# Average pooling over 8192 rows: larger loads, grouped stores and a last group cut into pieces

## The chip, the cores and the metric

The kernel runs on one core of a Trainium2 chip. The metric is the device time of one execution in microseconds (us), as a median of several runs. All results use runs in the fast state alone; the granted clock was 1.0 in every profile. The profile's span is about 2 us shorter than the device time; times inside a profile count from the start of its span. DVE is the vector engine, ACT the scalar engine, Pool is GpSimd, and SP is the engine that issues the loads.

## The reference

Each row of 4096 floats is averaged in 256 windows of 16:

```python
# x: (32, 256, 4096) float32, output_size = 256
for i in range(output_size):
    start = int(i * length / output_size)
    end = int((i + 1) * length / output_size)
    result[:, :, i] = np.mean(x[:, :, start:end], axis=-1)
```

There are 32 x 256 = 8192 rows. 134.2 MB are read and 8.4 MB written, and every element takes part in one addition.

## The kernel before

One tile is 128 rows, one row per partition. A tile is loaded (2 MB, 16 KB per partition), reduced on DVE, scaled on ACT and stored (128 KB, 1 KB per partition). There are 64 tiles and four buffers of each kind. SP issues the loads and ACT the stores.

```python
    xin = ctx.enter_context(tc.tile_pool(name="xin", bufs=4))
    res = ctx.enter_context(tc.tile_pool(name="res", bufs=4))

    for i in range(n_tiles):            # 64
        # ... r0, r1 = i * 128, (i + 1) * 128; nr = 128; K = 16; O = 256 ...
        xt = xin.tile([P, O, K], mybir.dt.float32)
        nc.sync.dma_start(out=xt[:nr], in_=x_flat[r0:r1].rearrange("p (o k) -> p o k", k=K))

        rt = res.tile([P, O], mybir.dt.float32)
        nc.vector.tensor_reduce(out=rt[:nr], in_=xt[:nr],
                                axis=mybir.AxisListType.X, op=mybir.AluOpType.add)
        ot = res.tile([P, O], mybir.dt.float32)
        nc.scalar.mul(out=ot[:nr], in_=rt[:nr], mul=inv_k)

        nc.scalar.dma_start(out=out_flat[r0:r1], in_=ot[:nr])
```

## Time and profile before

| what | value |
|---|---|
| device time, median | 345.52 us (345.41 to 345.62) |
| span of the profile | 343.8 us |
| DVE busy | 82% |
| steady traffic | 428 GB/s, DMA engines fully busy |
| from the last load's landing to the end of the span | 7.5 us |

The page of the kernel before, cut: busy time by engine, DMA share and rate in 40 slices, DMA queues, the chain that ended last, the costliest group and the DMA issues.

```profile
DVE 282.9 (82%) x64; ACT 27.9 (8%) x65; POOL 0.2 (0%) x4
...
DMA  8999999999999999999999999999999999999991
...
DMA packets 18437, 142.65 MB, mean 415 GB/s; under 512 B 2049, under 2 KB 10241, under 8 KB 10241
...
q1 hardware_dynamic: 9216, 134.22, 91.4%
q10 hardware_dynamic: 9216, 8.39, 7.0%
...
DMA xt<-in_x_dram 77%; DVE rt L48 21%; SPq L45 0%; ACT ot L55 0%; DVEq L48 0%
...
L48 DVE TENSOR_REDUCE rt<-xt 128x256 f32<-128x4096 f32 x64 | 282.9, 4420 | 58.0 <-DMA xt<-in_x_dram 58.0
...
xt<-in_x_dram SPq DMA_DIRECT2D x64, 2048.0 KB, 16.3
out_dram<-ot ACTq DMA_DIRECT2D x64, 128.0 KB, 10.2
```

The DMA row has a 9 in every slice but the first and the last: the DMA engines never rest. DVE is 82% busy, and the end of its group line says that it waited 58.0 us for loads. So DMA bounds the body. The two queues, q1 for loads and q10 for stores, take 91.4% and 7.0% of the engines' time, together nearly all of it. A load takes 16.3 us from issue to landing, although one lands every 5.2 us: about three are always queued.

Windows of the kernel before (stretch in us, its length, busy time of DVE, ACT and Pool, clock, DMA share, GB/s):

```profile
80.00:120.00 40.00, 33.71 (x9) 3.33 (x8) 0.00 (x0) 1.00 1.01 428
120.00:160.00 40.00, 33.69 (x9) 3.33 (x8) 0.00 (x0) 1.00 1.01 428
```

The end of the chain of waits of the kernel before (start in us, length in us, what):

```profile
320.05 16.29 DMA xt<-in_x_dram
...
336.43 4.43 DVE rt L48
340.86 0.02 issue
340.88 0.42 ACT ot L55
```

The last load lands at 336.34. Then one reduce, one scaling and one store follow in series. In the trace's records of single packets the last read packet ends at 336.00.

### The profile page before, as it was taken

How to read it: one execution, taken by the hardware profiler on the slowest of the kernel's cores; microseconds unless marked ns; L12 is line 12 of the kernel's file. 1: busy time of each engine (PE TensorE's matmuls, PEld its weight loads, DVE VectorE, ACT ScalarE, POOL GpSimd, SP SyncE). 2: the span in 40 equal slices, each digit the busy share in tenths (PEclk: the TensorE clock that was granted, in tenths of full speed). 3: DMA queues.
4: the chain of work that ended last, by engine and by line, in shares of the span. 5: the costliest groups of instructions: out<-in, count | busy, mean ns of one | idle time of the engine just before them, and what ended most of it. 6: DMA issues, size and time to landing. Idle time of an engine off the chain costs nothing.

```text
span 343.8 us, 484 instructions
## 1 busy us (share of the span) xinstructions
DVE 282.9 (82%) x64; ACT 27.9 (8%) x65; POOL 0.2 (0%) x4
## 2 busy tenths in 40 slices
DVE  0988988988888888889879889888888888898895
ACT  1000000000000000000000000000000000000000
POOL 0000000000000000000000000000000000000000
DMA  8999999999999999999999999999999999999991
GB/s 305 429 421 433 433 426 425 425 430 433 427 423 423 436 430 425 424 425 435 430 424 424 426 436 425 426 425 431 432 425 427 423 431 431 427 425 426 430 417 43
DMA packets 18437, 142.65 MB, mean 415 GB/s; under 512 B 2049, under 2 KB 10241, under 8 KB 10241
## 3 DMA queue, kind: packets, MB, share of 16 engines
q1 hardware_dynamic: 9216, 134.22, 91.4%
q10 hardware_dynamic: 9216, 8.39, 7.0%
q14 instruction: 5, 0.03, 0.0%
HBM read 134.22 MB, written 8.39 MB: 415 GB/s over the span
## 4 chain that ended last, share of the span: by engine, by line
DMA 77%; DVE 21%; issue 0%; SPq 0%; ACT 0%; DVEq 0%
DMA xt<-in_x_dram 77%; DVE rt L48 21%; SPq L45 0%; ACT ot L55 0%; DVEq L48 0%
## 5 line engine op out<-in xcount | busy, mean ns | idle before, releaser
L48 DVE TENSOR_REDUCE rt<-xt 128x256 f32<-128x4096 f32 x64 | 282.9, 4420 | 58.0 <-DMA xt<-in_x_dram 58.0
L55 ACT ACTIVATE ot<-rt 128x256 f32<-128x256 f32 x64 | 26.6, 416 | 312.7 <-DVE rt L48 312.7
L55 ACT ACT_TABLE_LOAD x1 | 1.3, 1283 | 0.7 <-PEq L74 0.7
L74 POOL MEMSET const-bfloat16-1.0<- 128x1 bf16 x1 | 0.1, 103 | 0.0
L74 POOL MEMSET const-uint8-127<- 128x1 uint8 x1 | 0.1, 102 | 0.0
L74 POOL MEMSET const-float32-0.0<- 128x1 f32 x1 | 0.1, 100 | 0.2 <-issue 0.2
L74 POOL MEMSET const-float32-1.0<- 128x1 f32 x1 | 0.1, 99 | 0.0
## 6 DMA issues: line engine op xcount, KB each, us to landing
xt<-in_x_dram SPq DMA_DIRECT2D x64, 2048.0 KB, 16.3
out_dram<-ot ACTq DMA_DIRECT2D x64, 128.0 KB, 10.2
```

The costliest lines, as they stand in the source:

```text
L48: nc.vector.tensor_reduce(out=rt[:nr], in_=xt[:nr], axis=mybir.AxisListType.X, op=mybir.AluOpType.add,)
L55: nc.scalar.mul(out=ot[:nr], in_=rt[:nr], mul=inv_k)
L74: nc = _bacc.Bacc("TRN2", target_bir_lowering=False, num_devices=1)
```

## The change

The intent is threefold. Eight neighbouring rows go to one partition, so that a load takes two rows per partition (32 KB, 4 MB in all). Eight rows of results are scaled by one instruction and stored by one transfer (8 KB per partition, 1 MB). The last group is cut so that little is left after the last load: 2 MB chunks, then nine pieces from 1 MB down to 128 KB, with stores in between.

```diff
+    R = 8
+    W = 2
+    S = R // W
+    x_g = x_flat.rearrange("(g p r) l -> g p (r l)", p=P, r=R)
+    o_g = out_flat.rearrange("(g p r) o -> g p (r o)", p=P, r=R)
     xin = ctx.enter_context(tc.tile_pool(name="xin", bufs=4))
-    res = ctx.enter_context(tc.tile_pool(name="res", bufs=4))
+    res = ctx.enter_context(tc.tile_pool(name="res", bufs=2))
 ...
+            # load_slot(s): W rows of every partition, one load, one reduce
+            xt = xin.tile([P, W * L], FP, name="xt")
+            nc.sync.dma_start(out=xt, in_=x_g[g, :, base:base + W * L])
+            nc.vector.tensor_reduce(out=rt[:, s * W * O:(s + 1) * W * O], ...)
 ...
+        def store(r0, r1):
+            nc.scalar.mul(out=ot[:, r0 * O:r1 * O], in_=rt[:, r0 * O:r1 * O], mul=inv_k)
+            nc.scalar.dma_start(out=o_g[g, :, r0 * O:r1 * O], in_=ot[:, r0 * O:r1 * O])
+
+        if not last:
+            for s in range(S):
+                load_slot(s)
+            store(0, R)
+        else:
+            for s in range(S - 2):
+                load_slot(s, tail_chunks=[L, L])
+            store(0, R - 4)
+            load_slot(S - 2, tail_chunks=[L, L])
+            store(R - 4, R - 2)
 ...
+            for ne in (L // 2, L // 4, L // 4):      # piece: load ne elements, reduce them
+                piece(e, e + ne); e += ne
+            store_cols(0, O)
+            for ne in (L // 4, L // 4):
+                piece(e, e + ne); e += ne
+            store_cols(O, O + O // 2)
+            for ne in (L // 4, L // 8, L // 16, L // 16):
+                piece(e, e + ne); e += ne
+            store_cols(O + O // 2, 2 * O)
```

(Cut and joined in places; the arithmetic is the same.)

More of the change, by code (lines that the diff above doesn't have):

```diff
@@ L19 @@
     P = nc.NUM_PARTITIONS
+    FP = mybir.dt.float32
     B, C, L = x.shape
@@ L31, with reduce_cols @@
     out_flat = out.flatten_outer_dims()
-    n_tiles = (rows + P - 1) // P
     inv_k = 1.0 / K
-    xin = ctx.enter_context(tc.tile_pool(name="xin", bufs=4))
-    res = ctx.enter_context(tc.tile_pool(name="res", bufs=4))
-    for i in range(n_tiles):
-        r0 = i * P
-        r1 = min(r0 + P, rows)
-        nr = r1 - r0
-        xt = xin.tile([P, O, K], mybir.dt.float32)
-        nc.sync.dma_start(out=xt[:nr], in_=x_flat[r0:r1].rearrange("p (o k) -> p o k", k=K))
-        rt = res.tile([P, O], mybir.dt.float32)
+    R = 8
+    W = 2
+    S = R // W
+    rows_per_group = P * R
+    n_groups = rows // rows_per_group
+    assert n_groups * rows_per_group == rows
+    x_g = x_flat.rearrange("(g p r) l -> g p (r l)", p=P, r=R)
+    o_g = out_flat.rearrange("(g p r) o -> g p (r o)", p=P, r=R)
+    xin = ctx.enter_context(tc.tile_pool(name="xin", bufs=4))
+    res = ctx.enter_context(tc.tile_pool(name="res", bufs=2))
+    def reduce_cols(xt, rt, r, cs, ce):
         nc.vector.tensor_reduce(
-            out=rt[:nr],
-            in_=xt[:nr],
+            out=rt[:, cs:ce],
+            in_=xt[:, cs * K:ce * K].rearrange("p (o k) -> p o k", k=K),
             axis=mybir.AxisListType.X,
@@ L53, with load_slot, piece, store_cols @@
         )
-        ot = res.tile([P, O], mybir.dt.float32)
-        nc.scalar.mul(out=ot[:nr], in_=rt[:nr], mul=inv_k)
-        nc.scalar.dma_start(out=out_flat[r0:r1], in_=ot[:nr])
+    for g in range(n_groups):
+        last = g == n_groups - 1
+        rt = res.tile([P, R * O], FP, name="rt", tag="rt")
+        ot = res.tile([P, R * O], FP, name="ot", tag="ot")
+        def load_slot(s, tail_chunks=None):
+            xt = xin.tile([P, W * L], FP, name="xt")
+            base = s * W * L
+            if tail_chunks is None:
+                nc.sync.dma_start(out=xt, in_=x_g[g, :, base:base + W * L])
+                nc.vector.tensor_reduce(
+                    out=rt[:, s * W * O:(s + 1) * W * O],
+                    in_=xt.rearrange("p (o k) -> p o k", k=K),
+                    axis=mybir.AxisListType.X,
+                    op=mybir.AluOpType.add,
+                )
+            else:
+                e0 = 0
+                for ne in tail_chunks:
+                    e1 = e0 + ne
+                    nc.sync.dma_start(
+                        out=xt[:, e0:e1], in_=x_g[g, :, base + e0:base + e1]
+                    )
+                    nc.vector.tensor_reduce(
+                        out=rt[:, s * W * O + e0 // K:s * W * O + e1 // K],
+                        in_=xt[:, e0:e1].rearrange("p (o k) -> p o k", k=K),
+                        axis=mybir.AxisListType.X,
+                        op=mybir.AluOpType.add,
+                    )
+                    e0 = e1
+                assert e0 == W * L
+        def store(r0, r1):
+            nc.scalar.mul(
+                out=ot[:, r0 * O:r1 * O], in_=rt[:, r0 * O:r1 * O], mul=inv_k
+            )
+            nc.scalar.dma_start(
+                out=o_g[g, :, r0 * O:r1 * O], in_=ot[:, r0 * O:r1 * O]
+            )
+        if not last:
+            for s in range(S):
+                load_slot(s)
+            store(0, R)
+        else:
+            for s in range(S - 2):
[3 more added lines that the diff above has]
+            store(R - 4, R - 2)
+            xt = xin.tile([P, W * L], FP, name="xt")
+            base = (S - 1) * W * L
+            rbase = (S - 1) * W * O
+            def piece(e0, e1):
+                nc.sync.dma_start(
+                    out=xt[:, e0:e1], in_=x_g[g, :, base + e0:base + e1]
+                )
+                nc.vector.tensor_reduce(
+                    out=rt[:, rbase + e0 // K:rbase + e1 // K],
+                    in_=xt[:, e0:e1].rearrange("p (o k) -> p o k", k=K),
+                    axis=mybir.AxisListType.X,
+                    op=mybir.AluOpType.add,
+                )
+            def store_cols(c0, c1):
+                nc.scalar.mul(
+                    out=ot[:, rbase + c0:rbase + c1],
+                    in_=rt[:, rbase + c0:rbase + c1],
+                    mul=inv_k,
+                )
+                nc.scalar.dma_start(
+                    out=o_g[g, :, (R - 2) * O + c0:(R - 2) * O + c1],
+                    in_=ot[:, rbase + c0:rbase + c1],
+                )
+            e = 0
+            for ne in (L // 2, L // 4, L // 4):
+                piece(e, e + ne)
+                e += ne
+            store_cols(0, O)
+            for ne in (L // 4, L // 4):
+                piece(e, e + ne)
+                e += ne
+            store_cols(O, O + O // 2)
+            for ne in (L // 4, L // 8, L // 16, L // 16):
+                piece(e, e + ne)
+                e += ne
+            assert e == W * L
+            store_cols(O + O // 2, 2 * O)
```

## The prediction

> **What bounds the kernel now.** DMA. The windows view gives a DMA share of 1.01 and about 428 GB/s (402.6 read, 25.1 written) in every steady stretch. DVE is busy 82% but waits on loads before every reduce (58.0 us, groups view). The chain of waits is 77% DMA; its 21% of DVE are reduces freeing buffers, harmless because 16.3 us of loads are always queued (issue to landing). Only the ends are serial: the last load lands at 336.34, then reduce 4.42, mul 0.42, store to the end at 343.85: 7.5 us of tail.
>
> **What changes.** The same 134.2 MB are read, 8.4 MB written and as many elements reduced.
>
> 1. Packets. The trace's packets are regular: 16 KB read 611 ns, 1 KB write 46 ns, 4 B semaphore 9 ns. The line through these has about 8 ns fixed per packet and a slope equal to 435 GB/s on 16 engines, the fabric ceiling in the Trainium skill, "DMA: Bandwidth & Descriptors", section Specifications. Before the first store, reads alone run at 431.2 GB/s; from that and the steady mix, writes are worth 380 GB/s. Stores of 8 KB per partition should go near 430: 2.6 us saved over 8.39 MB. If 32 KB rows go as one packet, the reads save up to 1.4 us more; if split at 16 KB, nothing. Estimate: 2.6 to 4 us off the DMA stream, all critical.
>
> 2. Tail. The last pieces are small (the last reduce is 128x256 elements), which looks like saving 4 us. I expect less, because DVE is nearly as slow as DMA: 4.45 us against 5.1 us per 2 MB. When the last 2 MB chunk before the pieces lands, DVE still owes it 4.45 us plus 8192 elements in nine reduces. With 1.04 ns an element (0.96 GHz, Trainium skill, "Trainium Kernel Development and Optimization", section NeuronCore Architecture; that leaves 0.15 of 4.42 us as fixed cost) these take about 10.3 us: 14.7 in all. DMA needs 9.7 us for the last 4 MB, 0.4 for the pieces' packets and some 1.6 for held-back stores: 11.8 us. So DVE ends about 3 us after the last load lands, not 0.5; before it was 4.5. The last mul and store are half as big: 0.1 us. Saving about 1.6 us.
>
> 3. No cost expected: the first reduce starts at about 13 us rather than 8.6, but DVE has slack (8.7 us per 10.3 us load), and four 4 MB buffers keep two loads queued. Fewer DMA issues and muls are off the path.
>
> Sum: 4.2 to 5.6 us off 345.5. Predicted 340.6 us (-1.4%), range 338.3 to 343.2. Faster by over 2% 0.13, within 2% 0.82, slower 0.05.
>
> **What would show it.** Step 1: steady windows at 430 to 433 GB/s; 8 KB write packets near 310 ns; about 7,900 packets, or 11,500 if split; last load landing at 332.5 to 334. Step 2: no DVE idle in the last 10 us, last reduce ending 2 to 4 us after the last landing; within 1 us, step 2 is wrong. Step 3: no DMA gap before the tail.
>
> **What would make it wrong.** Each partition's row in HBM now lies 128 KB from the next rather than 16 KB. The skill's DMA page (section Latency and other measured facts) shows large power-of-two pitches slowing DMA from 512 KiB up; no trace here shows one. If it bites at 128 KB, the kernel is slower. On the other side, bunched stores that make loads land later in the tail would let DVE catch up, saving 2 us more; and writes overlapping reads could lift the stream to 435 GB/s, just over the 2% line.

## The result

The changed kernel takes 340.66 us (340.47 to 340.80, 7 runs) against 345.52 us. The ratio is 0.9859, with a 95% interval of 0.9849 to 0.9869; that is clearly faster. Ratios in this document are the mean time of one kernel's fast runs over that of the other's fast runs of the same rounds, so they are not quite the ratio of the medians.

The page of the changed kernel, the lines that answer to those above:

```profile
DVE 278.5 (82%) x43; ACT 17.4 (5%) x13; POOL 0.2 (0%) x4
...
DMA  7999999999999999999999999999999999999994
...
DMA packets 7920, 142.61 MB, mean 421 GB/s; under 512 B 880, under 2 KB 1520, under 8 KB 2544
...
q1 hardware_dynamic: 6192, 134.22, 92.6%
q10 hardware_dynamic: 1728, 8.39, 6.0%
...
L67 DVE TENSOR_REDUCE rt<-xt 128x512 f32<-128x8192 f32 x28 | 243.2, 8686 | 55.4 <-DMA xt<-in_x_dram 55.4
...
xt<-in_x_dram SPq DMA_DIRECT2D x28, 4096.0 KB, 32.5
...
out_dram<-ot ACTq DMA_DIRECT2D x7, 1024.0 KB, 16.0
```

There are 7,920 packets in place of 18,437. The DMA engines are as full as before, DVE is as busy and waits as long. The body is bound by the same thing and moves its bytes a little faster. The same windows of the changed kernel:

```profile
80.00:120.00 40.00, 33.53 (x5) 1.91 (x1) 0.00 (x0) 1.00 1.00 433
120.00:160.00 40.00, 33.49 (x5) 1.91 (x1) 0.00 (x0) 1.00 1.00 433
```

The tail of the changed kernel, from its timeline (start, length, engine, line, operation, shapes, count, idle time before it):

```profile
321.94 4.42 DVE L80 TENSOR_REDUCE rt<-xt 128x256 f32<-128x4096 f32 x1 [0.68 <-DMA xt<-in_x_dram]
326.27 9.15 DVE L117 TENSOR_REDUCE rt<-xt 128x128 f32<-128x2048 f32 x9
...
335.46 0.31 ACT L125 ACTIVATE ot<-rt 128x128 f32<-128x128 f32 x1 [2.06 <-DVE rt L117]
335.80 0.34 ACTq L130 DMA_DIRECT2D out_dram<-ot  x1
```

Read the two DVE lines together. The reduce at 321.94 takes the last 2 MB chunk and waits 0.68 us for it. The nine reduces of the pieces follow with no idle time in brackets: their data was always there first. The last read packet ends at 333.32, the last reduce at 335.44, the span at 338.5. So the last 2.1 us of DVE work are a backlog, not a wait for the last piece. The trace's semaphore events say the same: the last piece was reported as landed at 333.76, and its reduce began at 335.02.

By the packet records, the last load came 2.7 us earlier (336.00 to 333.32) and the stretch behind it became 2.6 us shorter (7.8 to 5.2). The span fell by 5.3 us and the device time by 4.9; the gap between span and device time grew from 1.8 to 2.1 us. In the profiled runs below that gap is either 1.7 to 1.8 or 2.1 to 2.2 us (1.7 in `e8`, which has the same loads and stores), so it can't be put down to the change; nothing here explains it.

### The profile page after: what moved, and what is told of

Its sections match the earlier page's. It is cut to its first block, busy times and chain, and to the rows that moved or that the text cites. A ratio compares the mean times of both kernels' runs of the same rounds, so it can differ in the third digit from the quotient of the medians.

```text
span 338.5 us, 207 instructions
## 1 busy us (share of the span) xinstructions
DVE 278.5 (82%) x43; ACT 17.4 (5%) x13; POOL 0.2 (0%) x4
## 2 busy tenths in 40 slices
DMA packets 7920, 142.61 MB, mean 421 GB/s; under 512 B 880, under 2 KB 1520, under 8 KB 2544
## 4 chain that ended last, share of the span: by engine, by line
DMA 76%; DVE 22%; SPq 0%; DVEq 0%; issue 0%; ACT 0%
DMA xt<-in_x_dram 76%; DVE rt L67 18%; DVE rt L117 3%; DVE rt L80 1%; SPq L66 0%; DVEq L179 0%; SPq L77 0%; ACT ot L125 0%
## 5 line engine op out<-in xcount | busy, mean ns | idle before, releaser
L67 DVE TENSOR_REDUCE rt<-xt 128x512 f32<-128x8192 f32 x28 | 243.2, 8686 | 55.4 <-DMA xt<-in_x_dram 55.4
L90 ACT ACTIVATE ot<-rt 128x2048 f32<-128x2048 f32 (+2 forms) x9 | 15.1, 1673 | 310.0 <-DVE rt L67 285.2
L80 DVE TENSOR_REDUCE rt<-xt 128x256 f32<-128x4096 f32 x6 | 26.3, 4415 | 1.5 <-DMA xt<-in_x_dram 1.5
L117 DVE TENSOR_REDUCE rt<-xt 128x64 f32<-128x1024 f32 (+3 forms) x9 | 9.2, 1090 | 0.0
L125 ACT ACTIVATE ot<-rt 128x128 f32<-128x128 f32 (+1 forms) x3 | 1.0, 345 | 7.7 <-DVE rt L117 7.7
## 6 DMA issues: line engine op xcount, KB each, us to landing
xt<-in_x_dram SPq DMA_DIRECT2D x5, 512.0 KB, 15.8
```

Of the source, the lines that this page charges most:

```text
L67: nc.vector.tensor_reduce(out=rt[:, s * W * O:(s + 1) * W * O], in_=xt.rearrange("p (o k) -> p o k", k=K), axis=mybir.AxisListType.X, op=m ...
L80: nc.vector.tensor_reduce(out=rt[:, s * W * O + e0 // K:s * W * O + e1 // K], in_=xt[:, e0:e1].rearrange("p (o k) -> p o k", k=K), axis=my ...
L90: nc.scalar.mul(out=ot[:, r0 * O:r1 * O], in_=rt[:, r0 * O:r1 * O], mul=inv_k)
L117: nc.vector.tensor_reduce(out=rt[:, rbase + e0 // K:rbase + e1 // K], in_=xt[:, e0:e1].rearrange("p (o k) -> p o k", k=K), axis=mybir.Axis ...
L125: nc.scalar.mul(out=ot[:, rbase + c0:rbase + c1], in_=rt[:, rbase + c0:rbase + c1], mul=inv_k,)
```

## The experiments

Twelve kernels ran, all correct, each with the kernel before beside it (345.5 to 345.6 us in every round). Where packet times, landings or rates with two decimals are given, they come from the trace's records of single packets, with a packet's bytes spread evenly over its time. They are shown in tables, because the views give whole GB/s.

### Cutting only the tail of the kernel before

`e4` cuts the last tile of the kernel before into six pieces, `e5` the last two tiles into the same nine pieces that the change has. Nothing else is touched.

```diff
+        if i >= n_tiles - N_CUT:
+            for group in CUTS[i - (n_tiles - N_CUT)]:
+                # for each n of group: load n windows, reduce them; then scale and store the group
+    # e4: CUTS = [[[64, 64], [64, 32, 16, 16]]]
+    # e5: CUTS = [[[128, 64, 64]], [[64, 64], [64, 32, 16, 16]]]
```

> The kernel before with its last 2 MB tile alone cut into six loads, reduces and two stores; all else as before. Theory (DVE backlog): the tile ahead of it lands at 330.8 and its reduce ends at 335.65; then DVE works 4.75 us on the six pieces without a pause, last reduce at 340.4 against 340.86, half a store: about 345.0 us, DVE ending 4 us after the last load. Rival (only the last piece's reduce is serial): about 341.8 us.

> The kernel before with its last two tiles in the same nine pieces and three stores as the changed kernel's last slot. Theory (DVE backlog): the tile ahead has its reduce end at 330.4, the nine pieces take DVE 9.15 us as in the changed kernel, last reduce at 339.6, about 344.1 us. Rival (only the last piece's reduce is serial): about 341.8 us.

Measured: `e4` 344.90 us (ratio 0.9982, 0.9969 to 0.9994), `e5` 343.95 us (0.9952, 0.9940 to 0.9965). Both are as the backlog theory has it, and far from the 341.8 us of its rival. The timeline of `e4`:

```profile
331.20 4.42 DVE L71 TENSOR_REDUCE rt<-xt 128x256 f32<-128x4096 f32 x1 [0.79 <-DMA xt<-in_x_dram]
335.54 4.71 DVE L59 TENSOR_REDUCE rt<-xt 128x64 f32<-128x1024 f32 x6
```

DVE starts on the tile ahead at 331.20 and is not idle again until 340.25. The last read packet ended at 336.45, so 3.8 us of work were left at that moment, where the uncut kernel had 4.9 us until its reduce ended (336.00 to 340.86). DVE gains only some 0.8 us on DMA per 2 MB (the idle time of 0.79 in the first line), so cutting the last 2 MB cannot remove a backlog of one whole reduce. Cutting 4 MB removes more of it.

### Taking DVE work out of the tail

`e7` spreads the cuts over the whole last group. `e8` keeps the changed kernel and gives two pieces of 1024 elements to GpSimd, as four additions each.

```diff
 # e7: the last group
+            CUTS = [[[4096, 3584]], [[3072, 2560, 2048]], [[1024], [2048, 2048, 2048]],
+                    [[2048], [1536, 1536], [1024, 1024]], [[1024, 1024], [512, 256, 256]]]
 # e8: the second and the fourth piece
+                if pool:
+                    tree(e0, e1)      # four nc.gpsimd.tensor_tensor additions
+                    return
```

> The changed kernel with its whole last group in pieces that shrink slowly (4096 elements down to 256) and stores that follow. Theory (DVE backlog; smaller pieces leave less of it at each landing): last reduce ends about 1 us after the last landing rather than 2.1, about 339.7 us. Rival (the tail is bound by latency of landing and store, not by DVE): 340.7 us or slightly more for the extra packets.

> The changed kernel with two of the nine last pieces (1024 elements each) summed on GpSimd by four additions apiece, which takes 2.3 us of work from DVE and leaves loads and stores as they are. Theory (DVE backlog ends the kernel): the last reduce is then bound by the last landing, about 334.2 instead of 335.4, time about 339.4 us. Rival (landing and store latency): 340.7 us. If GpSimd takes longer than about 3 us for a piece, the middle store is late and the run says nothing of DVE.

Measured: `e7` 340.76 us (0.9859, 0.9846 to 0.9873), no gain. `e8` 340.00 us (0.9838, 0.9825 to 0.9852), about 0.65 us better than the changed kernel by the medians, half of what was expected; the two intervals overlap. By the spans of their profiles (338.3 and 338.5) it is only 0.2 us shorter; the rest lies in the unexplained gap between span and device time.

In `e7` the backlog did shrink, to 1.4 us behind the last read packet, but that packet came at 334.09 instead of 333.32. With 19 loads instead of 15 in the last group, the gain on DVE went back to DMA. Small pieces cost DMA time in the changed kernel too: from 327 to 330 us, where its pieces are 4 KB per partition, traffic runs at 409 GB/s.

The timeline of `e8`:

```profile
330.68 1.22 DVE L142 TENSOR_REDUCE rt<-xt 128x64 f32<-128x1024 f32 x1 [0.87 <-DMA xt<-in_x_dram]
...
332.34 2.46 DVE L142 TENSOR_REDUCE rt<-xt 128x64 f32<-128x1024 f32 x4 [0.44 <-DMA xt<-in_x_dram]
```

The brackets now have DMA in them: DVE waits for pieces, which it never did in the changed kernel. It ends at 334.80 instead of 335.44. So the backlog was what ended the changed kernel, and with it gone the last four pieces themselves, 2.5 us of reduces, are the next limit. A kernel with no pieces at all shows what they are for:

```diff
 # e3
-        last = g == n_groups - 1
+        last = False
```

> The changed kernel without its last-group branch: the last group is four 4 MB loads, one multiplication and one 1 MB store like the others. Theory: last load lands near 331 us (no 1 MB of stores before it), then reduce 8.7, multiplication 1.9, store issue 0.4 and 1 MB of store 4.5 us: span near 347 us, about 349 us, slower than the kernel before. Rival (the coarse body is what pays, the pieces do little): about 341 to 343 us.

Measured: 348.51 us (1.0084, 1.0071 to 1.0097), slower than the kernel before. Its last read packet ended at 330.96, earlier than in any other run, and 15.8 us of reduce, scaling and 1 MB store followed. The larger loads need the cut tail.

### Load size alone

`e1` is the changed kernel with 2 MB loads of one row per partition and eight buffers, and the same layout, stores and pieces. (Eight buffers of half the size hold as many bytes, but twice as many loads can be queued.)

```diff
-    W = 2
+    W = 1
-    xin = ctx.enter_context(tc.tile_pool(name="xin", bufs=4))
+    xin = ctx.enter_context(tc.tile_pool(name="xin", bufs=8))
     # ... and the last nine pieces in two tiles of one row instead of one of two
```

> The changed kernel with loads of one row per partition (16 KB packets, 2 MB a load, eight buffers), its stores and its last nine pieces as they are. Theory (fixed cost per packet): reads go back from 433.3 to 431.15 GB/s in the steady stretch, 134 MB then take 1.5 us more, about 342.2 us. Rival (only stores matter): 340.7 us, reads alone still at 433.

Measured: 342.87 us (0.9922, 0.9910 to 0.9934), 2.2 us over the changed kernel; expected were 1.5. Together with `e5` this gives a ladder from the kernel before to the changed one:

| kernel | median us | step |
|---|---|---|
| before | 345.52 | |
| `e5`: nine pieces at the end | 343.95 | -1.6 |
| `e1`: and eight-row layout, grouped 8 KB stores | 342.87 | -1.1 |
| changed: and 32 KB loads | 340.66 | -2.2 |

The packet records say where the last step comes from. Reads alone, from 13 to 30 us and so before any store, ran at 431.1 GB/s in 16 KB packets (`e1`) and 433.3 GB/s in 32 KB packets (changed). With stores, from 69 to 275 us:

```
                 reads   writes   together   (GB/s)
before           402.5     25.2     427.7
e1               403.7     25.1     428.9    (101 to 268 us)
changed          406.9     25.4     432.3
```

8 KB stores with 16 KB loads gain only 0.3%; 32 KB loads with the same stores gain 0.8% more. But these two steps are not cleanly separated, because `e1` has a slowness of its own. Still before any store, from 30 to 48 us, its reads fell to 428.5 GB/s, where the changed kernel kept 433.2. From 101 to 268 us its 16 KB packets lasted 613.9 ns on average, against 611.3 ns for the same packets in the kernel before; over 8192 packets on 16 engines that is an estimate of 1.3 us. So a part of the 2.2 us belongs to `e1` and not to the load size, and without it the 8 KB stores would have gained more than 0.3%. `e1` differs from the kernel before in its layout, its stores and its longer queue of loads (36.6 us from issue to landing in place of 16.3); which of them lengthens the packets is not shown.

Most packet durations fit one line: 46 ns for 1 KB, 84 for 2, 159 for 4, 309 for 8, 611 for 16 and 1213 for 32 KB. That line has 8.4 ns per packet and a slope equal to 435 GB/s on 16 engines, which agrees with the fabric ceiling that the Trainium skill gives ("DMA: Bandwidth & Descriptors", section Specifications).

### Store packets alone

Undoing the 8 KB store packets took two tries. `e2` sends every row's results as a transfer of its own:

```diff
-            nc.scalar.dma_start(out=o_g[g, :, r0 * O:r1 * O], in_=ot[:, r0 * O:r1 * O])
+            for r in range(r0, r1):
+                nc.scalar.dma_start(out=o_g[g, :, r * O:(r + 1) * O], in_=ot[:, r * O:(r + 1) * O])
```

> The changed kernel, each group's store sent as one store per row (1 KB packets) after the same one multiplication. Theory: writes go back from about 420 to 380 GB/s, 8.4 MB then take about 2 us more: the last load lands about 2 us later, 342.7 us. Rival (all of the stream's gain is from the 32 KB reads): 340.7 us.

Measured: 356.10 us (1.0299, 1.0286 to 1.0312), a loss of 15.4 us that no theory had. The edit changed more than the packet size. It added transfers. In the trace the landings of both queues come on eight semaphores, and the load queue waited 36.4 us for stores in the body, where the changed kernel has no such wait; that fits loads having to wait until an older store frees a semaphore. How its 15.4 us divide between this and the packets was not pursued. `e2b` keeps one transfer per store and forces 1 KB packets by padding the rows of the source in on-chip memory:

```diff
-        ot = res.tile([P, R * O], FP, name="ot", tag="ot")
+        ot3 = res.tile([P, R, O + 16], FP, name="ot", tag="ot")
 ...
-                out=o_g[g, :, r0 * O:r1 * O], in_=ot[:, r0 * O:r1 * O]
+                out=o_g[g, :, r0 * O:r1 * O].rearrange("p (r o) -> p r o", o=O),
+                in_=ot3[:, r0:r1, 0:O],
```

> The changed kernel with every store still one transfer, but its source in padded rows so that it is moved in 1 KB packets (rows of 256 outputs); number of transfers, and with it the sharing of DMA semaphores, is that of the changed kernel. Theory (fixed cost per packet): writes at about 380 GB/s in place of 420, last load lands about 2 us later, 342.7 us. Rival (1 KB packets themselves cost the 15 us of the run with one transfer per row): about 355 us.

Measured: 347.39 us (1.0050, 1.0036 to 1.0063), 6.7 us over the changed kernel; expected were 2. From its waits of the load queue (engine, line, what it waited for: us in total, times, longest us):

```profile
SPq L67 <- DMA out_dram<-ot: 97.4, 4, 32.1
```

From its DMA issues (what, queue, count, KB each, us to landing):

```profile
out_dram<-ot ACTq DMA_DIRECT2D x7, 1024.0 KB, 32.9
```

A 1 MB store took 32.9 us to land at the median, against 16.0 in the changed kernel, and loads waited 97.4 us for stores, against none in the body there. The packet records show both sides of it. From 58 to 120 us reads ran at 416.7 GB/s and writes at 14.5. From 122 to 124 us it was 0 and 387: the loads that should have been queued were waiting for the store. Near 198 us the engines ran half empty, at 132 and 177 GB/s. In the tail the loads waited for stores again, and DVE for pieces (3.7 us): of the 6.9 us by which the last reduce came later than in the changed kernel, 2.9 had arisen when the last 2 MB chunk landed and 4.0 came after it.

The cause that fits: the two queues take turns packet by packet. The Trainium skill says that each DMA engine goes round-robin between its queues at the granularity of packets ("DMA: Bandwidth & Descriptors", section Queues, rings and completion order). One 1 KB write per 32 KB read is 1 KB in 1213 + 46 ns on each of 16 engines, an estimate of 13 GB/s. The measured 14.5 is near it, and the kernel needs 25. (The page counts about 9 to 17 descriptors to a packet; the estimate takes one of the trace's packet records per turn, or equally many of each queue, and no run shows which.) With 16 KB reads the same estimate is 25 GB/s, just what is needed; that is the kernel before. The next run tests it with 2 KB packets, an estimate of 25 GB/s again:

```diff
-        ot3 = res.tile([P, R, O + 16], FP, name="ot", tag="ot")
+        ot2 = res.tile([P, R // 2, 2 * O + 16], FP, name="ot", tag="ot")
     # ... and the views of ot and of the output in rows of 2 * O
```

> As the run with stores in 1 KB packets in one transfer, but 2 KB packets. Theory (the two queues take turns packet by packet, so 32 KB of reads pass for every write packet: 1 KB gives writes about 13 GB/s where 25 are needed, 2 KB gives about 26): stores no longer pile up behind the loads, about 341.5 to 342 us. Rival (small write packets just cost time in proportion): about 344 us, half of the 6.7 us lost with 1 KB.

Measured: 340.14 us (0.9843, 0.9829 to 0.9856). The loss is gone at once, not by half, which is what taking turns predicts and a cost in proportion does not. While a store was under way (97 to 133 us) writes ran at 28 GB/s, near the estimate of 25. From its DMA issues and its waits of the load queue:

```profile
out_dram<-ot ACTq DMA_DIRECT2D x7, 1024.0 KB, 42.0
SPq L67 <- DMA out_dram<-ot: 53.8, 5, 12.9
```

So a late landing is not the harm by itself: at the median the stores landed even later here, after 42.0 us, and loads still waited for them. But the longest such wait in the body was 12.9 us, not 32.1, and the stream stayed full. The run is even 0.5 us below the changed kernel by the medians, with overlapping intervals. The stream in this run is slightly slower (431.5 GB/s) than the changed kernel's 432.3, but two other things are better. First, the reads do not slow down at the first store. In the changed kernel the rate fell to about 350 GB/s near 56 us, at the first store, and packets lost some 0.6 us there, and no later store did that; in this run it was 0.04 us. `e1`, `e3`, `e7` and `e8` slow down at their first 8 KB store too (by 0.3 to 0.8 us), but `e6` below, with 8 KB stores and another row pitch, does not (0.05 us). Why the first 8 KB store does this is open. Second, slower stores are held back longer, as the next section shows.

### The partition pitch

The prediction named one danger: a large power-of-two distance in HBM between one partition's data and the next. The change takes it from 16 KB to 128 KB. `e6` takes it to 1 MB (and that of the outputs from 8 to 64 KB).

```diff
-    x_g = x_flat.rearrange("(g p r) l -> g p (r l)", p=P, r=R)
-    o_g = out_flat.rearrange("(g p r) o -> g p (r o)", p=P, r=R)
+    x_g = x_flat.rearrange("(p g r) l -> g p (r l)", p=P, r=R)
+    o_g = out_flat.rearrange("(p g r) o -> g p (r o)", p=P, r=R)
```

> The changed kernel with all 64 rows of a partition next to each other in HBM: partitions lie 1 MB apart rather than 128 KB, everything else the same. Theory (no pitch effect for these loads): 340.7 us and 433 GB/s of reads. Rival (large power-of-two pitch slows loads, as the skill's DMA page has it from 512 KiB up): steady reads 3 to 20% slower, 350 us or more.

Measured: 343.54 us (343.09 to 344.58; 0.9944, 0.9932 to 0.9956), 2.9 us over the changed kernel and the widest spread of all runs. The loss is neither zero nor 3%: it lies in patches. In this profile reads fell to 350 to 400 GB/s near 13, 34, 43 and 126 us, and from 154 to 278 us the traffic was 432.3, as in the changed kernel. The first three of these patches came before any store, so they are the loads' own. At 128 KB the 32 KB packets showed no loss: reads alone ran at 433.3 GB/s, as in `e11` below, whose rows lie 32 KB apart (433.2 from 5 to 13 us). Whether the slower 16 KB packets of `e1` come from its 128 KB pitch is open. The skill ("DMA: Bandwidth & Descriptors", section Latency and other measured facts) has copies between HBM tensors falling from 207 GB/s per direction at a 512 KiB pitch to 164 at 2 MiB. These loads lost far less.

### Two closing kernels

`e10` joins `e9` and `e8`. `e11` keeps two rows per partition throughout: contiguous 4 MB loads, one 256 KB store of 2 KB packets after each, and the same cut tail.

```diff
 # e11
-    R = 8
+    R = 2        # a group is one load, one reduce, one scaling, one store; the last four groups are cut
```

> The 2 KB stores and the two pieces on GpSimd together. Theory (the stream and the tail add up): 340.66 less 0.5 less 0.65, about 339.5 us, last load at 333.1, last reduce at 334.4. Rival (one hides the other): 340.0 us.

> Two rows per partition throughout: 4 MB loads that are contiguous in HBM, one 256 KB store of 2 KB packets per load, the last four loads cut like those of the changed kernel. Theory (what matters is 32 KB loads, write packets of at least one part in sixteen of a read packet, and the cut tail; not grouping stores by eight rows): as the run with 2 KB packets in one transfer, 340.1 us, no slow reads near the first store. Rival (grouping stores is what pays): about 341.7 us, as e5's tail with only the loads' gain.

Measured: `e10` 340.20 us (0.9843, 0.9828 to 0.9857), `e11` 341.52 us (0.9883, 0.9866 to 0.9899). The gains of `e8` and `e9` do not add up, and `e9`, which groups by eight rows, is 1.4 us faster than `e11`, which does not. In `e10` the last read packet came at 333.59, 0.5 us later than in `e9`, with slower reads between 55 and 105 us, and DVE waited for its pieces there. No version clearly beats the changed kernel: the intervals of `e8`, `e9` and `e10` overlap with its own.

`e11` misses although its stream is as fast as `e9`'s (431.5 GB/s both). Five kernels with the same nine pieces, in none of which DVE waited for a piece, obey one rule, read from the packet records and the timelines:

| kernel | last 2 MB chunk landed | last reduce ended | difference | MB written after that chunk landed |
|---|---|---|---|---|
| `e5` | 325.53 | 339.45 | 13.9 | 0.61 |
| `e1` | 324.02 | 338.00 | 14.0 | 0.99 |
| `e11` | 322.41 | 336.61 | 14.2 | 0.72 |
| changed | 321.42 | 335.44 | 14.0 | 0.97 |
| `e9` | 320.79 | 334.70 | 13.9 | 1.15 |

Once the last 2 MB chunk has landed, DVE needs 14 us, as long as DMA brings the pieces in time. In `e2` and `e2b`, whose pieces waited behind stores, it was 15.3 and 18.0 us. Where the pieces do come in time, what counts is how early that chunk lands. Writes that are still outstanding then run beside the DVE backlog and are nearly free. Grouping by eight rows holds more of them back: 0.99 against 0.61 MB from `e5` to `e1`, which at 429 GB/s is an estimate of 0.9 us. The other part of that step is the 0.3% of the stream, another estimate of 0.9 us, less what the first store cost. `e11` holds 0.43 MB less than `e9`, an estimate of 1.0 of the 1.6 us by which its chunk came later.

## Why the prediction was right or wrong

The total was right: 340.6 us predicted, 340.66 measured. So was the mechanism. That the total is exact is partly luck: counted as the prediction counts, the stream saved less than the middle of its estimate, the tail 1 us more than its estimate, and the gap between span and device time took back the rest.

- **DMA bounds the body: right.** The windows moved from 428 to 433 GB/s with DMA share at 1.00 and DVE as idle as before.
- **The check marks: right but for one.** 8 KB packets took 309 ns, there were 7,920 packets (32 KB rows go unsplit), the last read packet ended at 333.32 and landed at 333.76, inside 332.5 to 334. But the last reduce was to end 2 to 4 us after the last landing, and it ended 1.7 us after it (2.1 after the last read packet).
- **"Stores of 8 KB per partition should go near 430: 2.6 us saved": somewhat too much.** By the prediction's own arithmetic, the changed kernel's steady mix (406.9 and 25.4 GB/s, against 433.3 for reads alone) makes writes worth about 417 GB/s in place of 380, an estimate of 2.0 us saved. `e1` shows less, a stream only 0.3% faster, but with slower reads of its own. 2 KB packets (`e9`) do as well.
- **"The reads save up to 1.4 us more": about right.** From 431.2 to 433.3 GB/s for reads alone is an estimate of 1.5 us. The 2.2 us between `e1` and the changed kernel are more than that, but they contain the slowness of `e1`.
- **"2.6 to 4 us off the DMA stream": at the low end.** The last read packet came 2.7 us earlier. The slow reads at the first store, 0.6 us, were not foreseen.
- **Tail, "saving about 1.6 us": too small.** The last reduce was to end 3 us after the last load's landing in place of 4.5; it ended 1.7 us after it, and the stretch behind the last read packet shrank by 2.6 us. DMA was to need 11.8 us for the last 4 MB and took 11.9 (321.42 to 333.32). The mis-sized term is "about 10.3 us" for the nine reduces, which took 9.15. The 1.04 ns an element is borne out (8686 ns for 8192 elements, 4415 for 4096), and with nine fixed costs of 0.15 it gives 9.9, not 10.3. The rest is overlap: one reduce of 1024 elements lasts 1.21 us, but the next starts 1.13 us after it, so that the fixed cost is half hidden. `e5`, which has the cut alone, gained 1.6 us in total; its last read packet came 0.5 us later, which hides a part of the tail's gain.
- **The mechanism of the tail: right.** `e4`, `e5` and `e8` each separate backlog from latency, and each sides with backlog.
- **No cost elsewhere: nearly right.** There is no gap, but reads slowed once near 56 us, at the first store, for 0.6 us. The gap between span and device time also grew by 0.3 us, as it does in some runs and not in others. Neither was foreseen and neither is explained.
- **The pitch: no harm at 128 KB in 32 KB packets;** `e6` shows that the worry was not empty at 1 MB.

## What to carry to other kernels

When two engines run at nearly the same pace, cutting the last tile into small pieces saves little: work out the backlog of the slower chain from the last large piece on, and shift that piece earlier, for example by holding back writes that can run beside the backlog. When loads and stores share DMA engines, give the stores packets at least as large, relative to the load packets, as their share of the bytes; below that they can starve and in the end stop the loads. Here stores were 1/16 of the bytes; beside 32 KB reads, 2 KB writes kept up and 1 KB writes did not. A prediction can be exact in its sum with terms that are off, so test the terms one by one, and check that the kernel that tests a term changes nothing else, which `e1` did not pass.

## What the Trainium skill lacked or had wrong

- "DMA: Bandwidth & Descriptors", section Queues, rings and completion order: it has the round-robin by packets, but not its consequence for unequal packets. With 32 KB reads and 1 KB writes, writes got 14.5 GB/s where 25 were needed, loads waited up to 32.1 us for a store, and the kernel lost 6.7 us; with 2 KB packets it lost nothing, though a store still took 42.0 us to land.
- The same page, Rules for kernel authors, asks for at least 1 MiB per transfer for the highest bandwidth. Going from 2 MB loads (16 KB per partition) to 4 MB (32 KB) still raised reads alone from 431.1 to 433.3 GB/s and the mixed stream from 428.9 to 432.3 (a part of the latter belongs to `e1`). The fixed cost read from the packets is 8.4 ns each, up to 32 KB; the page's own figures per packet are for small ones.
- The same page, Latency and other measured facts: its row of pitches starts at 512 KiB. Here 128 KB cost nothing in loads of 32 KB packets, and 1 MB cost 0.8% in passing patches (343.54 against 340.66 us).
- No page read for this case has the slowing of reads at the first 8 KB store (about 0.6 us, once, in the profile of the changed kernel; 0.3 to 0.8 us in `e1`, `e3`, `e7` and `e8`; none in `e6`).
